# The first layer's gate and FFN modulation vectors in two 16-bit parts, through tiles of their own

## The chip, the cores and the metric

The kernel runs on one core of one Trainium2 chip. The metric is device time in microseconds (us) of one execution. Three runs of the kernel before gave 1661.7, 1661.75 and 1665.76 us; their median, 1661.75 us, is the time before.

## The reference, cut to what matters

Two models run one after the other: a two-layer block (a mixer and a convolutional FFN in each layer, with modulation vectors), and then a hybrid block. The change touches only the modulation vectors of the first layer (layer 0, the "even" one):

```python
mod_l = (jax.nn.silu(c) @ mod_w[layer] + mod_b[layer])[:, None, :]
mod_c = (jax.nn.silu(c_ctx) @ mod_w[layer] + mod_b[layer])[None, None, :]
sh1l, sc1l, g1l, sh2l, sc2l, g2l = jnp.split(mod_l, 6, axis=-1)
...
yc, yl = even_mixer(hc, hl, ...)
xl = xl + g1l * yl
hl = modulate(xl, norm_ffn_g[layer], sh2l, sc2l)
xl = xl + g2l * conv_ffn(hl, ...)
```

Of the six vectors, numbered r = 0 to 5, the first two shape the mixer's input. Vector 2 is the gate on the mixer's output, 3 and 4 are shift and scale of the FFN's norm, 5 is the gate on the FFN's output. Each is a product of two input vectors (latent and context) of 1024 with a 1024 x 1024 matrix in 32-bit floats: 4 MB of weights a vector.

## The kernel before, in words

**Weights.** Weights arrive in 32-bit floats as tiles `st` of 128 x 2048 (1 MB), by `load_w` (L313), whose loads stand on SP's queue one after the other. For the large products `get_w` (L318) makes two 16-bit parts of a tile: `whi` is its rounding to f16 on ACT (through `act`, L306), `wlo` the remainder in bf16, a subtraction on DVE or, with `eng=self.G`, on GpSimd (through `tt`, L294). A product is then three passes of 16-bit matmuls (L332).

**Modulation.** `mod_steps` (L487) computes one vector of one layer in four blocks b, each with one 1 MB tile. With `whole=True` a block is 16 matmuls in 32-bit floats directly on `st`, with the 32-column input `cs` (L505). The trace records each of these as two, so a vector has 64 records. Without `whole` the block goes through `get_w`, and 16 matmuls, 8 on `whi` and 8 on `wlo`, run with the input in three bf16 pieces, `c3`. After the four blocks the row is copied out (`mrow`, ACT), transposed by two small matmuls (L514) and added to the bias (`modc`, DVE). The four matmuls of one k go to four separate groups of 32 columns of PE.

**The first layer's mixer.** `layer0_mixer` (L538) opens three pools, `gp` (the linear attention), `ev` (`yf`, `mqk`, `vext`) and `mp` (the mLSTM's work tiles), runs the mixer, and closes them. What follows uses their space: `xT` (the residual), and the pool `tw`, which holds the output projection's weight parts and the four `st` tiles of vector 5. Pools are made with `reuse_waits="tile"`, so that a new tile waits for the old tiles under it only. Under the last tiles of `tw` and behind them lie `yf`, `vext` and the tiles of `mp`, which are read until the mLSTM's last head is done.

**Around the change.** Vectors 2, 3 and 4 are computed with `whole=True`, their `st` tiles from the pool `wst` (three tiles, on the other side of the memory, used by all weight loads). Behind them in the program come the projection `eo` (four blocks `even_o`, 96 matmuls of 512 columns for the first two and 192 of 256 columns for the others), whose results are multiplied by vector 2 and added to `xT` (L303, DVE), the FFN's norm, vector 5, and the FFN's first product `up`.

**The order.** Tile's scheduler orders the instructions of each engine at build time, with the program's order as priority: what stands later in the program fills places where earlier work isn't ready. Once built, each engine and SP's queue run in that fixed order. So the matmuls of vectors 2 to 4, which stand behind the mixer in the program, are spread between the matmuls of the mLSTM (`S` L943, `nd` L956, `msk` and `plain` L928 to L930).

Of the kernel before, what the change touches and what calls it, by code (L numbers as in the profile page):

```python
# [248 lines left out]
class Program:  # L249
# [288 lines left out]
    def layer0_mixer(self):  # L538
        h, I = self.h, self.I
        with ExitStack() as ph:  # L540
            gp = self.pool("gp", 1, None, ph)
            ev = self.pool("ev", 1, None, ph)
            mp = self.pool("mp", 1, None, ph)
            yf = ev.tile([128, 8, 512], F32, name="yf")
            mqk = ev.tile([128, 8, 512], F32, name="mqk")
            vext = ev.tile([128, 4, 4, 129], F32, name="vext")
            self.rows = [mp.tile([128, 512], F32, name=n) for n in ("li", "lf", "lb", "lm")]
            for t in self.rows:
                self.G.memset(t[:64], 0.0)
            self.G.memset(vext[:, :, :, 128:129], 1.0)  # L550
            self.gla(gp, h, I["even_w"], yf)
            self.mlstm_inputs(h, I["even_w"], mqk, vext, yf)
            for i in range(4):
                self.split(h[0][:, i], h[1][:, i], yf[:, i])
            self.mlstm(mp, h, mqk, vext, yf)
            self.dbg("ym", h[0])
        self.res2 = self.pool("res2")
        self.xT = self.res2.tile([128, 8, 512], F32, name="xT")
        self.nc.sync.dma_start(self.xT, I["xT"].rearrange("p (k t) -> p k t", k=8))
        with ExitStack() as tail:  # L560
            tw = self.pool("tw", 4, None, tail)
            for r in (2, 3, 4):
                for _ in self.mod_steps(0, r, whole=True):
                    pass
            w = [self.get_w(I["even_o"][b], 4, 512, parts=tw) for b in range(4)]

            for b in range(2):
                for c in range(4):
                    ps = self.mm("eo")
                    self.proj_fm(ps, w[b], c * 128, 128, h, 0, 512, nk=4)  # L570
                    self.add_residual(ps, 0, 2, 4 * b + c, BOTH)

            for s in range(2):
                for b in range(2):
                    for c2 in range(2):
                        ps = self.mm("eo")
                        for c in range(2):
                            self.proj_fm(ps[:, c * 256:c * 256 + 256], w[2 + b], (2 * c2 + c) * 128, 128, h,
                                         256 * s, 256 * s + 256, nk=4, h0=4)
                        for c in range(2):  # L580
                            self.add_residual(ps[:, c * 256:], 0, 2, 4 * b + 2 * c2 + c, ((s, 0, 256),), 256 * s)
                if s == 0:
                    self.norm_stream(0, 1, 0, "ml")
            for _ in self.mod_steps(0, 5, pool=tw, whole=True):
                pass
        self.dbg("xmid0", self.xT)
# [1404 lines left out]
```

## Time and profile before

| | |
|---|---|
| median of three runs | 1661.75 us |
| the profiled execution's own time | 1664.73 us |
| its span, first to last instruction | 1662.9 us |
| PE busy | 1578.0 us (95%) |
| DVE busy | 1207.7 us (73%) |
| ACT busy | 848.6 us (51%) |
| POOL (GpSimd) busy | 490.0 us (29%) |
| mean granted TensorE clock | 0.977 |

PE's busy time counts matmuls from the first to the last of a run of them, with modelled ends, so a busy PE can still wait inside. The stretch that the change touches lies between 254 and 340 us of the span: the mLSTM's last units, the mixer's end, and the projection `eo`.

### The profile page before, as it was taken

How to read it: one execution, taken by the hardware profiler on the slowest of the kernel's cores; microseconds unless marked ns; L12 is line 12 of the kernel's file. 1: busy time of each engine (PE TensorE's matmuls, PEld its weight loads, DVE VectorE, ACT ScalarE, POOL GpSimd, SP SyncE). 2: the span in 40 equal slices, each digit the busy share in tenths (PEclk: the TensorE clock that was granted, in tenths of full speed). 3: DMA queues.
4: the chain of work that ended last, by engine and by line, in shares of the span. 5: the costliest groups of instructions: out<-in, count | busy, mean ns of one | idle time of the engine just before them, and what ended most of it. 6: DMA issues, size and time to landing. Idle time of an engine off the chain costs nothing.

```text
span 1662.9 us, 31811 instructions
## 1 busy us (share of the span) xinstructions
PE 1578.0 (95%) x12978; PEld 1083.3 (65%) x12978; DVE 1207.7 (73%) x2626; ACT 848.6 (51%) x1390; POOL 490.0 (29%) x275
## 2 busy tenths in 40 slices
PE   6999999899999999999899999599999999999998
PEld 3555865477444444376565667488887787778877
DVE  6877845778877795556887988899976875366734
ACT  4745524435555544434665565366664644556542
POOL 0000000035878740001000100279944312431150
PEclk9999999999999999999999999899999989999999
DMA  9322126642433446632222314345454342333651
GB/s 389 106 82 78 53 77 243 245 177 99 158 133 135 137 138 222 202 124 78 93 88 77 127 55 149 113 171 204 140 194 168 139 166 102 138 129 108 228 178 52
DMA packets 41186, 236.77 MB, mean 142 GB/s; under 512 B 4688, under 2 KB 5456, under 8 KB 21200
## 3 DMA queue, kind: packets, MB, share of 16 engines
q1 hardware_dynamic: 41040, 234.74, 40.0%
q8 instruction: 102, 1.67, 0.4%
q14 instruction: 44, 0.36, 0.1%
HBM read 233.68 MB, written 1.05 MB: 141 GB/s over the span
## 4 chain that ended last, share of the span: by engine, by line
PE 75%; DVE 11%; DMA 5%; ACT 5%; issue 3%; POOL 1%; ACTq 0%; SPq 0%; DVEq 0%; POOLq 0%
PE up L332 19%; PE sx L332 5%; PE dn L332 4%; PE fm L332 4%; PE mg L332 4%; PE mqk L332 3%; PE br L332 3%; DVE wlo L294 3%; PE tm L339 2%; ACT whi L306 2%; DMA st<-in_mod_w_dram 2%; PE sz L332 2%; PE eo L332 2%; PE so L332 2%; PE sc L1654 2%
## 5 line engine op out<-in xcount | busy, mean ns | idle before, releaser
L332 PEld LDWEIGHTS <-whi 128*128 128x128 f16 (+2 forms) x5240 | 511.9, 99 | 253.9 <-issue 38.7
L294 POOL TENSOR_TENSOR wlo<-st,whi 128x1024 bf16<-128x1024 f32 (+2 forms) x112 | 356.8, 3196 | 915.9 <-ACT whi L306 814.5
L306 ACT ACTIVATE whi<-st 128x2048 f16<-128x2048 f32 (+3 forms) x242 | 369.7, 1536 | 268.2 <-PE up L332 44.8
L332 PEld LDWEIGHTS <-wlo 128*128 128x128 bf16 (+2 forms) x2620 | 258.9, 99 | 126.0 <-issue 13.2
L303 DVE SCALAR_TENSOR_TENSOR u<-up,fcw,u 128x189 f32<-128x189 f32 (+3 forms) x792 | 297.6, 430 | 50.8 <-ACT u L306 42.7
L294 DVE TENSOR_TENSOR wlo<-st,whi 128x2048 bf16<-128x2048 f32 (+3 forms) x130 | 255.0, 1965 | 87.9 <-ACT whi L306 83.0
L332 PE MATMUL up<-hh,whi 128*128 128x256 f16 (+1 forms) x752 | 239.4, 320 | 2.7 <-ACT hh L306 1.9
L332 PE MATMUL up<-hl,whi 128*128 128x256 bf16 (+1 forms) x752 | 238.9, 319 | 2.7 <-DVE hl L303 2.7
L332 PE MATMUL up<-hh,wlo 128*128 128x256 f16 (+1 forms) x752 | 238.7, 319 | 0.0
L332 PE MATMUL dn<-hidh,wlo 128*128 128x256 f16 (+1 forms) x396 | 122.4, 311 | 2.0 <-DVE wlo L294 2.0
L332 PE MATMUL dn<-hidh,whi 128*128 128x256 f16 (+1 forms) x396 | 122.3, 310 | 0.9 <-ACT whi L306 0.7
L332 PE MATMUL dn<-hidl,whi 128*128 128x256 bf16 (+1 forms) x396 | 122.3, 310 | 0.0
L306 ACT ACTIVATE u<-up,ppt,fcw 128x512 f32<-128x512 f32 (+1 forms) x88 | 57.9, 659 | 44.0 <-PE up L332 43.9
L332 PE MATMUL fm<-hh,whi 128*128 128x256 f16 x288 | 78.5, 273 | 0.5 <-DVE xc L303 0.5
L332 PE MATMUL fm<-hh,wlo 128*128 128x256 f16 x288 | 78.5, 273 | 0.0
L332 PE MATMUL fm<-hl,whi 128*128 128x256 bf16 x288 | 78.5, 273 | 0.0
L332 PE MATMUL mg<-hh,wlo 128*128 128x256 f16 x256 | 71.0, 277 | 3.6 <-POOL wlo L294 3.6
L332 PE MATMUL mg<-hl,whi 128*128 128x256 bf16 x256 | 70.9, 277 | 1.2 <-DVE hl L303 1.2
L332 PE MATMUL mg<-hh,whi 128*128 128x256 f16 x256 | 70.7, 277 | 0.9 <-ACT mgt L306 0.9
L298 POOL TENSOR_SCALAR E<-E,rs 128x128 f32<-128x128 f32 (+1 forms) x48 | 37.1, 787 | 111.6 <-DVE rs L1665 51.1
L339 PEld LDWEIGHTS <-hh 128*128 128x128 f16 x640 | 62.8, 101 | 10.0 <-issue 1.1
L294 POOL TENSOR_TENSOR sg<-sg,u 128x512 f32<-128x512 f32 (+1 forms) x44 | 46.6, 1059 | 27.0 <-ACT sg L306 26.7
(539 smaller groups left out, 3075.2 us busy)
## 6 DMA issues: line engine op xcount, KB each, us to landing
st<-in_w_up_dram SPq DMA_DIRECT2D x44, 1024.0 KB, 4.9
st<-in_w_dram SPq DMA_DIRECT2D x25, 1024.0 KB, 4.8
st<-in_mod_w_dram SPq DMA_DIRECT2D x48, 512.0 KB, 4.5
st<-in_w_dn_dram SPq DMA_DIRECT2D x32, 704.0 KB, 4.1
st<-in_ssd_w_dram SPq DMA_DIRECT2D x20, 1024.0 KB, 4.8
st<-in_mod_w_dram SPq DMA_DIRECT2D x16, 1024.0 KB, 5.0
st<-in_w_m_dram SPq DMA_DIRECT2D x32, 512.0 KB, 4.3
st<-in_even_w_dram SPq DMA_DIRECT2D x14, 1024.0 KB, 5.1
```

Of the source, the lines that this page charges most:

```text
L294: (eng or self.V).tensor_tensor(o, a, b, op=op)
L298: (eng or self.V).tensor_scalar(o, a, s1, None, op0=op0)
L303: self.V.scalar_tensor_tensor(o, a, s, b, op0=op0, op1=op1)
L306: self.S.activation(o, i, func, **kw)
L332: self.T.matmul(ps, w[a][:, k, c0:c0 + cw], h[b][:, h0 + k, t0:t1], start=first and k == 0 and i == 0, stop=last and k == nk - 1 and i == 2)
L339: self.T.matmul(ps, h[b][:, k, t0:t0 + 128], w[a][:, k, c0:c0 + cw], start=k == 0 and i == 0, stop=k == nk - 1 and i == 2)
L1654: T.matmul(ps[:, a:b], q[r, tb * 128:tb * 128 + 128], k[r, 0:b - a], start=True, stop=False)
```

## The change

Vectors 2, 3 and 4 leave the 32-bit path. Their 12 blocks go through `get_w` with a pool `tm` of their own, two tiles each of `st`, `whi` and `wlo` (8, 4 and 4 KB a partition), opened behind `tw`; `wlo` is made on GpSimd. `tm` lies on the space of the closed pools: its first `st` tile is on the end of `vext` and the start of `mp`, the other tiles on `mp`.

```diff
@@ -559,8 +559,9 @@
         with ExitStack() as tail:
             tw = self.pool("tw", 4, None, tail)
+            tm = self.pool("tm", 2, None, tail)
             for r in (2, 3, 4):
-                for _ in self.mod_steps(0, r, whole=True):
+                for _ in self.mod_steps(0, r, eng=self.G, pool=tm, parts=tm):
                     pass
             w = [self.get_w(I["even_o"][b], 4, 512, parts=tw) for b in range(4)]
```

The scheduler then orders the program anew. Three places show it; line numbers behind L559 are one higher in the changed kernel.

**PE, from the last mLSTM unit on.** `nd` is the last unit's product, `yT` the transposition of a head's result, `mod` the modulation (L505), `eo` the projection. Before:

```order
L505 MATMUL mod<-st,cs 32x256 x10
L956 MATMUL nd<-vext,W 128x129 x14
L505 MATMUL mod<-st,cs 32x256
L943 MATMUL S<-mqk 128x256
L919 MATMUL yT<-ept,hm 128x128 x4
L943 MATMUL S<-mqk 128x256
L514 MATMUL mod<-ept,mrow 128x8 x2
L956 MATMUL nd<-vext,W 128x129 x20
L919 MATMUL yT<-ept,hm 128x128 x4
L332 LDWEIGHTS whi
L332 MATMUL eo<-hh,whi 128x512
```

Of the change:

```order
L957 MATMUL nd<-vext,W 128x129 x17
L944 MATMUL S<-mqk 128x256
L920 MATMUL yT<-ept,hm 128x128 x4
L944 MATMUL S<-mqk 128x256
L957 MATMUL nd<-vext,W 128x129 x20
L920 MATMUL yT<-ept,hm 128x128 x8
L505 LDWEIGHTS c_99
L505 MATMUL mod<-whi,c_99 32x256
```

All 192 matmuls of the three vectors now stand behind the last `nd` and `yT`. The 128 of vectors 2 and 3, and the first 8 of vector 4, stand ahead of the first `eo`; the rest of vector 4 stands in groups of 16 and 12 between groups of 12 `eo`.

**SP's queue from the end of the mixer's weights on** (`in_mod_w` 128x2048 are modulation weights of layer 0, `in_mod_w` 128x1024 those of layer 1, `in_w_up` the FFN's). Before:

```order
L315 DMA st<-in_even_w_dram 128x2048 x9
L315 DMA st<-in_mod_w_dram 128x2048 x3
L559 DMA xT<-in_xT_dram 128x4096
L315 DMA st<-in_mod_w_dram 128x2048 x9
L315 DMA st<-in_even_o_dram 128x2048 x3
L315 DMA st<-in_mod_w_dram 128x2048 x4
L315 DMA st<-in_even_o_dram 128x2048
L315 DMA st<-in_w_up_dram 128x2048 x2
L315 DMA st<-in_mod_w_dram 128x1024 x2
```

Of the change:

```order
L315 DMA st<-in_even_w_dram 128x2048 x9
L315 DMA st<-in_even_o_dram 128x2048 x3
L559 DMA xT<-in_xT_dram 128x4096
L315 DMA st<-in_mod_w_dram 128x2048 x4
L315 DMA st<-in_even_o_dram 128x2048
L315 DMA st<-in_w_up_dram 128x2048 x2
L315 DMA st<-in_mod_w_dram 128x2048 x2
L315 DMA st<-in_w_up_dram 128x2048 x3
L315 DMA st<-in_mod_w_dram 128x2048 x2
L315 DMA st<-in_w_up_dram 128x2048
L315 DMA st<-in_mod_w_dram 128x2048 x8
```

In both, the group of four `in_mod_w` tiles ahead of the last `even_o` is vector 5. The 12 tiles of vectors 2 to 4 stood ahead of `even_o`; now they stand behind the fourth `even_o` and two `w_up` tiles, two, two and eight at a time.

**POOL's subtractions from its first on.** The numbers tell the tiles apart: `st_4520`, `st_4576` and `st_4632` are `w_up`, the others here are `tm`'s, in order. Before, the first row was `wlo` of `w_up` too, with the two `w_up` tiles followed by layer 1's modulation. Of the change:

```order
L294 TENSOR_TENSOR wlo_4523<-st_4520,whi_4522 128x2048
L294 TENSOR_TENSOR wlo_4579<-st_4576,whi_4578 128x2048
L294 TENSOR_TENSOR wlo_3667<-st_3664,whi_3666 128x2048
L294 TENSOR_TENSOR wlo_3689<-st_3686,whi_3688 128x2048
L294 TENSOR_TENSOR wlo_4635<-st_4632,whi_4634 128x2048
L294 TENSOR_TENSOR wlo_3711<-st_3708,whi_3710 128x2048
L294 TENSOR_TENSOR wlo_3733<-st_3730,whi_3732 128x2048
L294 TENSOR_TENSOR wlo_3761<-st_3758,whi_3760 128x2048
```

Fifteen subtractions of 128x2048 stand in a row: three of `w_up` and the 12 of the three vectors.

## Rows read from the trace of the kernel before

**Rows 1.** The page: busy time by engine, and the chain by engine.

```profile
PE 1578.0 (95%) x12978; PEld 1083.3 (65%) x12978; DVE 1207.7 (73%) x2626; ACT 848.6 (51%) x1390; POOL 490.0 (29%) x275
PE 75%; DVE 11%; DMA 5%; ACT 5%; issue 3%; POOL 1%; ACTq 0%; SPq 0%; DVEq 0%; POOLq 0%
```

**Rows 2.** Windows: busy us by engine, PE's clock, DMA share, GB/s.

```profile
254.00:300.00 46.00, 46.00 (x365) 26.68 (x364) 25.65 (x104) 19.02 (x64) 0.00 (x0) 1.00 0.68 252
300.00:313.00 13.00, 8.18 (x58) 6.70 (x56) 11.04 (x47) 6.64 (x22) 0.00 (x0) 1.00 0.25 83
375.00:392.00 17.00, 17.00 (x158) 15.19 (x156) 10.46 (x36) 4.71 (x11) 0.00 (x0) 1.00 0.01 2
```

**Rows 3.** The chain between 254 and 317 us: shares, then pieces (start, us).

```profile
by line: PE nd L956 27.3%; PE mod L505 23.8%; PE S L943 13.8%; DVE wlo L294 3.7%; DVE W L303 2.9%; ACT whi L306 2.9%; ACT W L306 2.7%; DVE hm L303 2.7%; PE msk L930 2.6%; PE msk L928 2.6%; PE msk L929 2.5%; PE plain L929 2.5%; PE plain L928
262.71 3.12 PE nd L956 x28
278.45 3.32 PE nd L956 x28
296.51 2.67 PE nd L956 x22
306.88 3.41 PE nd L956 x28
```

**Rows 4.** Timeline at the mixer's end: DVE's last read of `yf`, and SP.

```profile
311.95 0.69 DVE L303 SCALAR_TENSOR_TENSOR hm<-yf,hm 128x512 f32<-128x512 f32 x1
312.74 2.37 SPq L315 DMA_DIRECT2D st<-in_mod_w_dram  x4
317.46 0.33 SPq L315 DMA_DIRECT2D st<-in_even_o_dram  x1
319.74 2.60 SPq L315 DMA_DIRECT2D st<-in_w_up_dram  x2
```

**Rows 5.** Timeline behind it: ACT's casts and POOL's first subtraction.

```profile
328.17 1.91 ACT L306 ACTIVATE whi<-st 128x2048 f16<-128x2048 f32 x1 [9.46 <-DMA st<-in_even_o_dram]
330.67 1.91 ACT L306 ACTIVATE whi<-st 128x2048 f16<-128x2048 f32 x1
332.65 4.08 POOL L294 TENSOR_TENSOR wlo<-st,whi 128x2048 bf16<-128x2048 f32 x1 [295.94 <-ACT whi L306]
```

**Rows 6.** The price of a block elsewhere: POOL's subtraction, all of POOL's, DMA to landing.

```profile
513.87 4.08 POOL L294 TENSOR_TENSOR wlo<-st,whi 128x2048 bf16<-128x2048 f32 x1 [2.16 <-ACT whi L306]
L294 POOL TENSOR_TENSOR wlo<-st,whi x112: 2114/3306/4524, 332.7 to 1621.1; 128x2048 bf16<-128x2048 f32 x54, 128x1024 bf16<-128x1024 f32 x54, 128x1408 bf16<-128x1408 f32 x4
st<-in_mod_w_dram SPq DMA_DIRECT2D x16, 1024.0 KB, 5.0
```

**Rows 7.** PE's timeline: `eo` from its start to the last of 512 columns.

```profile
310.68 0.66 PE L919 MATMUL yT<-ept,hm 128*128 128x128 f32 x4 [0.41 <-DVE hm L303]
315.17 0.61 PE L332 MATMUL eo<-hh,whi 128*128 128x512 f16 x1 [3.83 <-ACT whi L306]
320.45 0.45 PE L332 MATMUL eo<-hh,whi 128*128 128x512 f16 x1
338.88 0.38 PE L332 MATMUL eo<-hl,whi 128*128 128x512 bf16 x1
339.09 0.38 PE L332 MATMUL eo<-hh,wlo 128*128 128x512 f16 x1
```

**Rows 8.** The chain behind: `up`, and eight 16-bit modulation matmuls of layer 1.

```profile
375.22 17.14 PE up L332 x157
392.36 0.33 PE mod L505 x8
```

## The prediction

> **What bounds the kernel now.** I read the page first: PE is busy 95% of the span and 75% of the chain is PE's, while POOL is busy 29% [rows 1]. An average says little about the stretch that the change touches, so I took the windows there [rows 2]. From 254 to 300 us PE is busy throughout, at full clock; the reader is to see DVE at 25.65 of 46 us and ACT at 19.02 beside it. From 300 to 313 us PE has 8.18 of 13 us and DVE 11.04: the last mLSTM unit is a dependence between engines. The chain of the stretch [rows 3] gives the modulation's matmuls 23.8% of 63 us, 15.0 us, all between 254 and 297. Last come the timelines at the mixer's end [rows 4, 5, 7]. They show an end mark: DVE reads `yf` for the last time until 311.95 + 0.69 = 312.64. I call this moment M. SP's next load starts at M + 0.1, and `eo` starts at M + 2.5.
>
> **What is removed: PE's 32-bit matmuls in the mixer.** 15.0 us of PE leave the chain, and 0.6 us of L514's. How much sooner does the mixer end? At most 15.6, if PE alone bounds. Nothing, if these matmuls only fill places where PE would wait. The rows lie between. The last products of a head start at 262.71, 278.45, 296.51 and 306.88 [rows 3]: units of 15.7 and 18.1 us with modulation in them, and a last one of 10.4 us without any, which has no successor beside it. Two units of 12 us would save 9.8 us. Against 254 to 300 in full: with 15 us gone, DVE's 25.65 us would fill 83% of what is left, about as dense as in the last unit (11.04 of 13, 85%), where dependences set the pace [rows 2]. I take **10 us**, nearer to the units' own rows, with 3 and 15.6 for the range. M moves from 312.6 to about 302.6.
>
> **What is added: a chain of 12 blocks behind M.** PE is in order, and 128 modulation matmuls now stand ahead of the first `eo`. `eo` can't start before the eighth block's `wlo`. Nothing of a block can start before M: `tm`'s loads stand on SP behind the fourth `even_o` and two `w_up` loads, each of which waits for a DVE subtraction that itself comes behind the mixer. I take their times from the same loads of before, M + 4.8, M + 7.1 and M + 9.4 (319.74 + 2.60 less the 0.33 of an issue) [rows 4]. The first two `tm` loads so start at M + 9.7, behind 4 MB of vector 5 and 3 MB more. But POOL is not ready for them anyway:
>
> - POOL's first `w_up` subtraction starts at M + 20.0 (332.65) [rows 5], as before, since what leads to it is the same. Then come `w_up`, two blocks, `w_up`, two blocks. Seven subtractions of 4.08 us [rows 6] end at M + 48.6, with block 4.
> - Block 5's `st` comes free with block 3's `wlo`, M + 44.5. Its load lands 5.0 us later [rows 6], and I add 0.1 since a `w_up` load runs ahead of it; ACT casts in 1.9 us [rows 5], POOL subtracts in 4.1: block 5 at M + 55.7, and block 6, loaded from M + 48.6, at M + 59.8 behind it.
> - From here two tiles of `st` set the pace: load, cast, subtraction and 0.1 for the handovers, 5.0 + 1.9 + 4.1 + 0.1 = 11.1 us for a pair of blocks. Blocks 7 and 8 end at M + 66.8 and M + 70.9, 9 and 10 at M + 77.9 and M + 82.0, 11 and 12 at M + 89.0 and M + 93.1.
> - PE's part is small. Eight 16-bit matmuls take 0.33 us [rows 8], a block 0.66, and only the last 0.35 of the last block lies on the path. ACT's 12 casts, 12 x 1.9 = 22.9 us, lie in the chain above; DVE gains nothing to do.
> - By M + 93.1 four groups of 12 `eo` have run between the blocks. 48 are left, at 339.09 - 338.88 = 0.21 us each: 10.1 us. PE has been idle most of the time, and so starts slow: after 3.83 us of idle time before, `eo` ran at 0.61 us a matmul until 320.45 instead of 0.38, half the clock for 5.3 us, which cost about 2.5 [rows 7]. End of the 512-column `eo`: 93.1 + 0.4 + 10.1 + 2.5 = M + 106.1.
>
> Before, the same `eo` end at 339.09 + 0.2 = 339.3, M + 26.7 [rows 7].
>
> **The sum.** 106.1 - 26.7 = 79.4 later, less the 10 by which M itself is earlier: 69.4, **70 us slower**. I see nothing behind that takes it back: the FFN's `up` runs from 375 to 392 with PE busy 17.00 of 17 us [rows 2, 8], so weights prepared longer ahead of it shorten nothing, and layer 1's modulation comes in the same lockstep as before. The sum was made in the profiled execution, whose 1664.73 us are 0.2% above the median of 1661.75; against the median it gives 1661.75 + 70 = 1732.
>
> **Two rules against the rows.** All of POOL's subtractions ran between 2.1 and 4.52 us [rows 6] over three widths; those of 2048 columns shown singly took 4.08 [rows 5, 6]. By the Trainium skill, "GPSIMD Engine Reference", section 3.1, a two-input operation of 2048 32-bit columns takes 4497 ns on GpSimd and 2293 ns on VectorE, and by the same page's section 8 it contends with VectorE's two-input instructions for its ports. By 4.5 instead of 4.08 the blocks would end about 12 x 0.4 = 5 us later, and the sum would be an estimated 75. The row decides for 4.08, since DVE has little to do while POOL works here.
>
> The clock after idle time is rows 7's. By the Trainium skill, "TensorE: Matmul & The Clock Gate", section "HAM oscillation — how this bites in real kernels", waits between bursts bring the half clock back every time. By it the `eo` between the blocks would run at half clock as well, which hides in POOL's time, and only the start of the last 48 counts, as in the sum.
>
> **The rivals.**
>
> *The blocks start before the mixer ends (faster).* A new tile waits only for the old tiles under it; if `tm`'s tiles came free early and loads and subtractions ran beside the mLSTM, PE would be rid of 15.6 us and `eo` would start as before: 1661.75 - 10 = 1652, at best 1646. It decides where block 8's `wlo` is done by M + 2.5, nearly 70 us sooner than above. For it speaks that POOL is idle in all of the mixer [rows 2, 5]. Against it: the tiles lie on `vext` and `mp`, read to the end, and SP's order holds them behind loads that start at M + 4.8 and later. Chance 0.03.
>
> *Loads are hidden, POOL alone is the bound.* Then 15 subtractions run without a gap from M + 20.0: 15 x 4.09 = 61.3, M + 81.3, 11.8 less than above: 58 slower, 1720. For this a load and a cast would have to fit beside one subtraction, 6.9 against 4.1 us [rows 5, 6]. If the mixer also ends the full 15.6 sooner, 1714. Chance 0.10.
>
> *POOL and PE are slower than their rows.* POOL at its largest 4.52 us [rows 6]: 5 us more; the last 48 `eo` all at half clock: 10.1 instead of 2.5 lost, 8 more; the mixer only 3 us sooner: 7 more. 70 + 20 = 90 slower, 1752. For it speaks that PE stops and starts twelve times here. Chance 0.14.
>
> *The time comes back behind, or the change does nothing.* If weight loads that now run ahead unblocked `up`, the end could be near 1662. The rows of `up` show no wait for weights [rows 8], and the built order does hold the 12 blocks. Chance 0.01.
>
> **How the numbers follow.** The forecast, 60 to 80 us slower, has a chance of 0.72. The range adds the near halves of POOL alone and of slower engines: 1715 to 1748. About 0.3%, 5 us, is what a measurement here can tell from no change. Faster by more: 0.03, the first rival. Within: 0.01. Slower: 0.96.
>
> **What would show it.** In the profile after: no L505 on `st` before 300 us, units of about 12 us in the mLSTM and M near 303; then PE nearly idle for some 70 us with its clock at half, and 15 POOL subtractions of 4.1 us, first without gaps, then two to every 11 us; the first `eo` at about M + 73. It is wrong if a `tm` load starts before M, if the pairs come closer than 10 us, or if `up` starts less than 55 us later than at 375.

## The result, and the profile after

Four runs of the changed kernel gave 1717.34 to 1732.42 us, median **1723.33 us**; four of the kernel before 1661.7 to 1665.84, median 1663.76. The ratio is 1.0361, with a 95% interval of 1.0329 to 1.0392: 60 us slower. The forecast was 1732, range 1715 to 1748. The profiled execution of the changed kernel took 1720.71 us, its span is 1718.8 us.

The page of the changed kernel, busy time by engine and the chain by engine, against [rows 1]:

```profile
PE 1565.8 (91%) x12912; PEld 1080.9 (63%) x12978; DVE 1204.8 (70%) x2626; ACT 871.5 (51%) x1402; POOL 539.6 (31%) x287
PE 70%; DVE 13%; ACT 5%; DMA 5%; issue 4%; POOL 3%; ACTq 0%; SPq 0%; DVEq 0%; POOLq 0%
```

POOL's busy time grew by 49.6 us, 12 subtractions of 4.1, as it had to. The number to see is its share of the chain, 1% before and 3% now. The chain between 254 and 440 us gives POOL's subtractions 17.8%, 33 us in which the end of the kernel waits for one of them. An engine's busy time says nothing of this.

The windows, with the columns of [rows 2]:

```profile
254.00:290.00 36.00, 31.04 (x172) 20.60 (x172) 27.12 (x110) 19.77 (x68) 0.00 (x0) 1.00 0.01 1
303.00:375.00 72.00, 14.11 (x148) 8.48 (x150) 9.72 (x15) 29.41 (x18) 47.81 (x12) 0.50 0.77 290
```

The mixer's end has lost the full PE of [rows 2], and its DMA share is 0.01: nothing is loaded beside it any more. Behind it stand 72 us in which PE works 14.11 us at a granted clock of 0.50, the lower of its two levels (1.2 of 2.4 GHz), while POOL works 47.81. That second row is the result.

DVE's last read of `yf` and SP's queue behind it, against [rows 4]:

```profile
297.88 0.69 DVE L303 SCALAR_TENSOR_TENSOR hm<-yf,hm 128x512 f32<-128x512 f32 x1
298.65 1.98 SPq L315 DMA_DIRECT2D st<-in_mod_w_dram  x4
305.67 2.60 SPq L315 DMA_DIRECT2D st<-in_w_up_dram  x2
308.32 0.90 SPq L315 DMA_DIRECT2D st<-in_mod_w_dram  x2
```

M is now 297.88 + 0.69 = 298.57, 14.07 us sooner than before. The first two tiles of `tm` are asked for at 308.32, M + 9.75. All of POOL's timeline up to the 12th block:

```profile
318.08 28.18 POOL L294 TENSOR_TENSOR wlo<-st,whi 128x2048 bf16<-128x2048 f32 x7 [280.01 <-ACT whi L306]
349.28 8.08 POOL L294 TENSOR_TENSOR wlo<-st,whi 128x2048 bf16<-128x2048 f32 x2 [3.03 <-ACT whi L306]
360.36 8.08 POOL L294 TENSOR_TENSOR wlo<-st,whi 128x2048 bf16<-128x2048 f32 x2 [3.00 <-ACT whi L306]
371.53 8.09 POOL L294 TENSOR_TENSOR wlo<-st,whi 128x2048 bf16<-128x2048 f32 x2 [3.09 <-ACT whi L306]
382.50 8.10 POOL L294 TENSOR_TENSOR wlo<-st,whi 128x2048 bf16<-128x2048 f32 x2 [2.89 <-ACT whi L306]
```

Seven subtractions without a gap, and then pairs that start 11.0 to 11.2 us apart with 3 us of idle time ahead of each. The bracket names ACT as the releaser, but ACT had itself waited. The chain of waits between 254 and 440 us shows one period whole:

```profile
338.18 4.07 POOL wlo L294
342.26 4.93 DMA st<-in_mod_w_dram
347.29 1.92 ACT whi L306
349.28 1.79 POOL wlo L294
```

Subtraction, load into the tile that it freed, cast, subtraction: the two `st` tiles in turn. Last, PE's `eo` against [rows 7], and the first long piece of `up` in the chain against [rows 8]:

```profile
373.19 0.59 PE L332 MATMUL eo<-hh,whi 128*128 128x512 f16 x1 [0.33 <-DVE modc L294]
386.62 0.29 PE L505 MATMUL mod<-wlo,c 128*32 128x256 bf16 x4 [1.16 <-POOL wlo L294]
391.09 0.39 PE L332 MATMUL eo<-hh,whi 128*128 128x512 f16 x1
402.39 0.38 PE L332 MATMUL eo<-hh,wlo 128*128 128x512 f16 x1
437.13 16.81 PE up L332 x154
```

`eo` starts at M + 74.6, the 512-column `eo` end at 402.6, M + 104.0, and that piece of `up` starts 61.9 us later than at 375.22. The first matmul of `up` is a sharper mark than the end: 368.4 us before, 430.0 now, 61.6 later. Behind it the ten profiled executions of this study take between 1284.5 and 1295.3 us to the end of their spans, in no order that follows the size of the edit's effect. So a median can be off by some us in either direction, and the mark is used beside the medians below.

### The profile page after: what moved, and what is told of

It is laid out like the page before. It is cut to its first block, busy times and chain, and to the rows that moved or that the text cites. A ratio compares the mean times of both kernels' runs of the same rounds, so it can differ in the third digit from the quotient of the medians.

```text
span 1718.8 us, 31781 instructions
## 1 busy us (share of the span) xinstructions
PE 1565.8 (91%) x12912; PEld 1080.9 (63%) x12978; DVE 1204.8 (70%) x2626; ACT 871.5 (51%) x1402; POOL 539.6 (31%) x287
## 4 chain that ended last, share of the span: by engine, by line
PE 70%; DVE 13%; ACT 5%; DMA 5%; issue 4%; POOL 3%; ACTq 0%; SPq 0%; DVEq 0%; POOLq 0%
PE up L332 17%; PE dn L332 7%; PE sx L332 5%; PE fm L332 4%; POOL wlo L294 3%; PE mg L332 3%; DVE u L303 3%; ACT whi L306 3%; PE sz L332 2%; DVE wlo L294 2%; PE br L332 2%; PE so L332 2%; PE eo L332 2%; DMA st<-in_w_m_dram 2%; PE tm L339 2%
## 5 line engine op out<-in xcount | busy, mean ns | idle before, releaser
L294 POOL TENSOR_TENSOR wlo<-st,whi 128x1024 bf16<-128x1024 f32 (+2 forms) x124 | 405.8, 3284 | 926.6 <-ACT whi L306 822.0
L306 ACT ACTIVATE whi<-st 128x2048 f16<-128x2048 f32 (+3 forms) x254 | 392.9, 1555 | 293.2 <-DMA st<-in_mod_w_dram 62.0
L332 PE MATMUL up<-hl,whi 128*128 128x256 bf16 (+1 forms) x733 | 230.4, 316 | 3.5 <-DVE hl L303 3.5
L332 PE MATMUL dn<-hidl,whi 128*128 128x256 bf16 (+1 forms) x384 | 117.0, 306 | 0.0
L505 PEld LDWEIGHTS <-c 128*32 128x32 bf16 x576 | 13.9, 101 | 83.7 <-issue 83.0
```

The lines of the kernel that those rows point to most:

```text
L294: (eng or self.V).tensor_tensor(o, a, b, op=op)
L306: self.S.activation(o, i, func, **kw)
L332: self.T.matmul(ps, w[a][:, k, c0:c0 + cw], h[b][:, h0 + k, t0:t1], start=first and k == 0 and i == 0, stop=last and k == nk - 1 and i == 2)
L505: T.matmul(ps[32 * j:32 * j + 32, :256], c[:, 2 * b + k], w[:, 0 if halves else k, 256 * j:256 * j + 256], start=b == k == i == 0, stop=b ...
```

## The experiments

The runs of the kernel before on the same chips had medians of 1663.8 (the first four experiments), 1665.1 (the next three) and 1663.4 us (the last). What they gave, with M and the first matmul of `up` from the traces:

| kernel | median us | ratio (95%) | M | first `up` |
|---|---|---|---|---|
| before | 1663.8 | 1 | 312.6 | 368.4 |
| the change | 1723.3 | 1.0361 (1.0329 to 1.0392) | 298.6 | 430.0 |
| 1, `wlo` on DVE | 1715.7 | 1.0306 (1.0248 to 1.0363) | 297.0 | 421.1 |
| 2, four half tiles | 1717.0 | 1.0310 (1.0238 to 1.0382) | 299.0 | 422.7 |
| 3, the place alone | 1706.2 | 1.0249 (1.0186 to 1.0312) | 297.1 | 411.9 |
| 4, the parts alone | 1680.5 | 1.0105 (1.0041 to 1.0168) | 328.5 | 391.5 |
| 5, the parts alone, DVE | 1671.6 | 1.0046 (1.0026 to 1.0067) | 320.4 | 377.4 |
| 6, vectors left out | 1645.2 | 0.9897 (0.9860 to 0.9935) | 296.6 | 352.1 |
| 7, two vectors behind `eo` | 1691.6 | 1.0173 (1.0141 to 1.0205) | 302.0 | 398.7 |
| 8, casts only | 1667.1 | 1.0019 (0.9990 to 1.0049) | 314.9 | 371.8 |

The diffs are against the changed kernel, in 5 and 8 against experiment 4's. The theory: the tiles' **place** puts a chain of 12 blocks behind M, and the two `st` tiles pace it, load, cast and subtraction one behind the other. The rivals: POOL's rate alone is the bound; the place alone costs it all; the parts alone do.

### 1. The subtraction on DVE

```diff
-                for _ in self.mod_steps(0, r, eng=self.G, pool=tm, parts=tm):
+                for _ in self.mod_steps(0, r, pool=tm, parts=tm):
```

> The same pool and order, wlo of the 12 blocks on DVE instead of GpSimd. Theory (two st tiles set the pace: load, cast, subtraction one behind the other, and POOL only through its 4.07 us): a pair of blocks takes 4.93 + 1.91 + 2.29 + 0.1 = 9.2 us instead of the 11.1 of the changed kernel, and the first two blocks no longer queue behind POOL's w_up, so the 12th ends near M + 74 instead of M + 92: about 18 us less than the changed kernel, 1705 us (1698 to 1712). Rival 1 (the rate of the subtracting engine alone is the bound): 12 x 2.29 = 27.5 us behind M + 25, M + 52, about 40 us less, 1683 us. Rival 2 (the place alone, whatever engine subtracts): no change, 1723 us. Periods between subtractions in the trace tell: 9.2 us a pair, 4.6 us a pair, or 11.1 us a pair.

Measured: 1715.68 us, outside the range. Pieces of the chain show two periods:

```profile
337.38 4.91 DMA st<-in_mod_w_dram
342.37 1.92 ACT whi L306
344.31 2.30 DVE wlo L294
346.63 4.81 DMA st<-in_mod_w_dram
351.55 1.92 ACT whi L306
353.49 2.30 DVE wlo L294
```

344.31, 353.49, then 362.72 and 371.93: 9.2 us a pair, as the theory has it. Both rivals' periods, 4.6 and 11.1, are out. The 12th block ends at 377.2, M + 80.2, not M + 74. The first pair was late, and its timeline shows why:

```profile
321.46 7.49 DVE L294 TENSOR_TENSOR wlo<-st,whi 128x2048 bf16<-128x2048 f32 x2 [5.19 <-ACT whi L306]
327.00 5.88 POOL L294 TENSOR_TENSOR wlo<-st,whi 128x2048 bf16<-128x2048 f32 x1 [2.39 <-ACT whi L306]
```

Two subtractions of 2.29 us on DVE took 7.49 while POOL worked on `w_up`, and one of 4.07 on POOL took 5.88 while DVE worked. I had not expected that the two engines hold each other up; experiment 4 shows it at length. The next pair was another 1.3 us late, as its load took 6.24 us. The last group of 12 `eo` ahead of the 12th block's matmuls then started only at 375.07, behind a DVE addition to `xT` that itself stood behind the 11th block's subtraction, and at half clock it took 4.31 us in place of 2.6. So the 512-column `eo` ended 16.5 us behind the 12th block, where the change has 12.0. These 6.2 and 4.5 us, less 1.6 by which M is sooner, are what is missing at `up`, which starts 8.9 us sooner than in the change where 18 were expected.

### 2. Four tiles of half the width

```diff
-            tm = self.pool("tm", 2, None, tail)
+            tm = self.pool("tm", 4, None, tail)
...
-                for _ in self.mod_steps(0, r, eng=self.G, pool=tm, parts=tm):
+                for _ in self.mod_steps(0, r, eng=lambda: self.G, pool=tm, parts=tm, halves=True):
```

> The same 32 KB a partition, but as four tiles of 1024 columns instead of two of 2048, wlo on GpSimd. Theory: with four tiles in turn a load (4.4 us to landing for 512 KB) and a cast (1.05) fit beside three subtractions of about 2.1 to 2.3 us, so POOL runs without gaps: 24 x 2.2 + 3 x 4.08 = 65 us behind M + 19.5, the last block at M + 84.5 instead of M + 92: 7 to 8 us less than the changed kernel, about 1716 us (1711 to 1720). This is what the prediction's second rival (POOL alone the bound) needs in order to hold. Rival (the loads' rate is the bound, not their turn with two tiles): gaps between POOL's subtractions stay, no change, 1723 us or more.

Measured: 1716.98 us, and 7.3 us less at `up`. POOL's timeline is one row for everything:

```profile
318.42 62.26 POOL L294 TENSOR_TENSOR wlo<-st,whi 128x2048 bf16<-128x2048 f32 x27 [279.97 <-ACT whi L306]
```

27 subtractions (three of `w_up`, 24 halves) without a gap, ended at M + 81.7. With four tiles the prediction's second rival is true, and POOL alone is the bound; with the change's two tiles it is not. The difference between the two is the 3 us ahead of each of the change's last four pairs, 12.0 us, less 1.7 that the halves take longer in all: the chain ends 10.3 us sooner.

### 3. The place alone

```diff
-                for _ in self.mod_steps(0, r, eng=self.G, pool=tm, parts=tm):
+                for _ in self.mod_steps(0, r, pool=tm, whole=True):
```

> The 32-bit path of the kernel before (no cast, no subtraction), but its st tiles from the pool on the closed mixer pools' space: the place alone. Theory (the blocks can't begin before DVE's last read of yf, and each pair of tiles waits for its use): M as in the changed kernel, 14 us sooner than before; a pair takes 4.93 us of load and up to 2.5 us of matmuls at half clock, 7.5 us, six pairs from M + 10 end at M + 55 instead of M + 92: 38 us less than the changed kernel, about 1685 us (1675 to 1697), still 11 to 35 us slower than the kernel before. Rival 1 (casts and subtractions are the whole cost, the place nothing): 1664 - 14 = 1650 us. Rival 2 (the place is the whole cost): 1723 us.

Measured: 1706.15 us, above the range: without any cast or subtraction the place still costs 43.5 us at `up`, more than two thirds of the change's 61.6. Pieces of the chain, and the windows (columns as in [rows 2]; the last three are PE's clock, DMA share and GB/s):

```profile
306.83 12.62 DMA st<-in_mod_w_dram
319.50 1.98 PE mod L505 x16
321.49 7.93 DMA st<-in_mod_w_dram
...
331.47 8.38 DMA st<-in_mod_w_dram
...
341.88 4.80 DMA st<-in_mod_w_dram
```

```profile
303.00:340.00 37.00, 9.97 (x76) 4.14 (x80) 8.05 (x12) 8.86 (x7) 12.14 (x3) 0.50 1.01 422
```

I had put 4.93 us on every load. That held for the next two on the chain (4.80 and 4.81 us), whose pairs came 6.8 and 6.9 us apart; a last one took 5.91. From 303 to 340 all 16 DMA engines were busy (1.01) at 422 GB/s, since vector 5, `even_o`, `w_up` and the moved 12 MB are all wanted at once. The first loads on the chain took 12.62, 7.93 and 8.38 us there, 14 us more in all than I had put. The place alone thus has a second cost: it moves 12 MB out of a stretch where little else is loaded (DMA share 0.01 in the change) into one where DMA is full.

### 4. The parts alone

```diff
-            tm = self.pool("tm", 2, None, tail)
...
-                for _ in self.mod_steps(0, r, eng=self.G, pool=tm, parts=tm):
+                for _ in self.mod_steps(0, r, eng=self.G):
```

> The 16-bit parts with wlo on GpSimd, but in the shared pools that the other weights use, so the loads can run beside the mixer: the parts alone. Theory (the place is what lets the chain show): the matmuls stand among the mixer's again, eo follows the mixer at once as in the kernel before, PE's modulation in the mixer falls from 15.0 to about 192 x 0.33 / 8 = 7.9 us, while ACT gains 12 x 1.9 = 23 us there beside its 19 of 46 us: between 7 us faster and 11 us slower than the kernel before, 1663 us (1655 to 1675), 50 us or more less than the changed kernel. Rival (12 subtractions of 4.07 us on GpSimd cost about their sum wherever they stand): 1700 us or more.

Measured: 1680.53 us, 43 less than the change, so the place is the larger part. But it is above the theory's range, and M is at 328.5, 16 us later than before, though PE's modulation fell from 18.31 us (window 240 to 312 of the kernel before) to 12.07 (240 to 330 here, the same 204 records). A vector's 64 records of the 32-bit path are 32 matmuls, eight a block and not 16 as I wrote in the description of the kernel. Two groups of DVE's instructions between 200 and 330 us, here:

```profile
L294 DVE TENSOR_TENSOR den<-den,guard 128x2 f32<-128x2 f32 x14 | 14.1, 1005 | 0.0
L298 DVE TENSOR_SCALAR den<-den 128x2 f32<-128x2 f32 x13 | 11.8, 907 | 0.3
```

and in the kernel before:

```profile
L298 DVE TENSOR_SCALAR den<-den 128x2 f32<-128x2 f32 x16 | 2.6, 167 | 0.2
L294 DVE TENSOR_TENSOR den<-den,guard 128x2 f32<-128x2 f32 x16 | 2.5, 157 | 9.3 <-ACT den L306 8.9
```

The same instructions on two columns take 5.4 and 6.4 times as long on average. DVE's and POOL's timelines beside each other say when:

```profile
269.92 3.47 DVE L294 TENSOR_TENSOR den<-den,guard 128x2 f32<-128x2 f32 x1
273.63 3.78 DVE L298 TENSOR_SCALAR den<-den 128x2 f32<-128x2 f32 x1
282.01 0.17 DVE L294 TENSOR_TENSOR modc<-mod,ept 128x16 f32<-128x16 f32 x1 [1.22 <-PE mod L514]
287.29 3.94 DVE L303 SCALAR_TENSOR_TENSOR r<-rt,r 128x4 f32<-128x4 f32 x1
309.86 0.69 DVE L847 TENSOR_REDUCE hss<-hsq 128x4 f32<-128x512 f32 x1 [0.47 <-ACT hsq L306]
```

```profile
265.27 12.11 POOL L294 TENSOR_TENSOR wlo<-st,whi 128x2048 bf16<-128x2048 f32 x3 [4.35 <-ACT whi L306]
280.78 4.06 POOL L294 TENSOR_TENSOR wlo<-st,whi 128x2048 bf16<-128x2048 f32 x1 [3.40 <-ACT whi L306]
287.14 4.07 POOL L294 TENSOR_TENSOR wlo<-st,whi 128x2048 bf16<-128x2048 f32 x1 [2.30 <-ACT whi L306]
309.39 8.09 POOL L294 TENSOR_TENSOR wlo<-st,whi 128x2048 bf16<-128x2048 f32 x2 [2.37 <-PE nd L956]
```

POOL's three subtractions from 265.27 end at 269.3, 273.4 and 277.4. DVE's `den` ends at 273.39, the next held one at 277.41, and `r` at 291.23 against POOL's 291.21: each held instruction ends with POOL's. Not all are held. While POOL ran, `modc`, one of whose two inputs is PE's result `mod`, took 0.17 us and the reduction `hss`, with one input, 0.69. By the Trainium skill, "SBUF — State Buffer", section "Who interferes with whom", GpSimd shares a pair of ports with VectorE under an exclusive lock that whoever issues first keeps for its whole instruction: a VectorE instruction with two SBUF inputs, or a one-input one in a two-port mode, which `tensor_scalar` can enter, is blocked until a GpSimd instruction that reads SBUF is done, and `tensor_reduce` never is. The trace agrees in every row above, and experiment 5 tests it.

### 5. The parts alone, subtracted on DVE

```diff
-                for _ in self.mod_steps(0, r, eng=self.G):
+                for _ in self.mod_steps(0, r):
```

> As the run with the parts in the shared pools (1680.53 us, M at 328.5), but wlo of the 12 blocks on DVE: the same 12 casts on ACT, 12 x 2.29 = 27.5 us more on DVE, nothing on POOL inside the mixer. Theory (GpSimd's subtractions hold up DVE: in that run a den of 0.16 us took 3.0 to 3.8 us and ended with POOL's subtraction): DVE's small instructions keep their 0.16 us, the mixer ends at least 8 us sooner, M between 306 and 320, time 1656 to 1672 us, in spite of more work on DVE. Rival (the casts on ACT and the longer way from load to matmul slow the mixer): M stays at 328 or later, 1680 us or more; with 27.5 us of DVE added to a full DVE up to 1690 us.

Measured: 1671.59 us, M at 320.4. DVE has 27.5 us more to do, and the mixer ends 8.1 us sooner than with POOL:

```profile
L298 DVE TENSOR_SCALAR den<-den 128x2 f32<-128x2 f32 x16 | 2.5, 165 | 0.1
L294 DVE TENSOR_TENSOR den<-den,guard 128x2 f32<-128x2 f32 x16 | 2.4, 157 | 2.9 <-ACT den L306 2.8
```

The small instructions are back at 157 and 165 ns. The hold-up was real: it cost 8.1 us at M, 14.1 at `up`, and 8.9 between the two medians. But M is 0.4 us past the theory's range: against the kernel before, 7.8 us remain that POOL doesn't explain.

### 6. The three vectors left out

```diff
-            tm = self.pool("tm", 2, None, tail)
...
-                for _ in self.mod_steps(0, r, eng=self.G, pool=tm, parts=tm):
-                    pass
+                self.V.memset(self.modc[0][:, r], 0.5)
+            self.stt(self.modA[0][:, 1], self.modc[0][:, 4], 1.0, bc(self.ng[1][:, 0], 1, 2), ALU.add, ALU.mult)
```

> Vectors 2, 3 and 4 left out: their rows are set to a constant, with no loads, casts, subtractions or matmuls. It measures by itself what the mixer gains when its 15.0 us of 32-bit matmuls go, and what the tail costs without any chain. Theory: M at 297 to 299 as in the changed kernel (14 to 15.6 us sooner than 312.6), eo at M + 2.5 and ended at M + 26.7 as before, so 14 to 16 us less than the kernel before: 1649 us (1644 to 1654); the chain of 12 blocks then costs 1723 - 1649 = 74 to 77 us. Rival (the mixer's end is freed but the time is lost again behind, in weights that come later than eo): over 1655 us.

Measured: 1645.17 us. M is 296.6, 16.0 us sooner, and `up` starts 16.3 us sooner: what the mixer gains reaches `up` whole. So a version of these three vectors has about 16 us to gain at `up`; the ratio of 0.9897 says 17 us of 1665, its interval 11 to 23. And the changed kernel's chain costs 430.0 - 352.1 = 77.9 us against having none.

### 7. Shift and scale behind the first `eo`

```diff
-            for r in (2, 3, 4):
-                for _ in self.mod_steps(0, r, eng=self.G, pool=tm, parts=tm):
-                    pass
+            for _ in self.mod_steps(0, 2, whole=True):
+                pass
...
+            for r in (3, 4):
+                for _ in self.mod_steps(0, r, eng=self.G, pool=tm, parts=tm):
+                    pass
             for s in range(2):
```

> Vector 2 on the 32-bit path in the mixer as before; vectors 3 and 4 through tm on GpSimd as in the changed kernel, but called behind the 512-column eo, so that no eo of 512 columns stands behind their matmuls on PE. Theory (a chain of 8 blocks that ends at M + 71 as in the changed kernel, whose end now holds the 256-column eo and the norm in place of the first eo): M about 10 us sooner than before, the 512-column eo ended near M + 27, the last eo some 10 us behind block 8, at M + 82 instead of M + 50: 32 less 10, about 22 us slower than the kernel before, 1686 us (1677 to 1696). Rival 1 (only PE's order held eo; behind it the chain is covered by eo): 1655 to 1664 us. Rival 2 (each block costs its share wherever it is called, 8 of 12): 1664 + 40 = 1704 us.

Measured: 1691.61 us, in the theory's range. M came 10.7 us sooner for two of three vectors. POOL's last pair and DVE's `sq` (of the FFN's norm) beside it:

```profile
364.80 8.27 POOL L294 TENSOR_TENSOR wlo<-st,whi 128x2048 bf16<-128x2048 f32 x2 [2.86 <-ACT whi L306]
365.06 8.29 DVE L294 TENSOR_TENSOR sq<-sq,s 128x256 f32<-128x256 f32 x2 [0.27 <-ACT s L306]
```

Block 8 ends at 373.07, M + 71.1, against the M + 71 expected and the M + 69.9 of the changed kernel: the chain's end hangs on M and the number of blocks, not on what PE does beside it. But `up` is 30.3 us late, not 22, since the last `eo` ran until M + 90.7. In the row of `sq`, two instructions that take 0.95 us for both once POOL is quiet took 8.29 beside POOL's 8.27: the hold-up of experiment 4, and the chain runs through both of them. The next 24 `eo` start behind them, at 374.19, at half clock (5.29 us, where the 24 after that take 2.79).

### 8. Casts without subtractions

```diff
-                terms = [(self.c3, w) for w in self.get_w(src, 2, 1024, eng, pool, parts)]
+                if l == 0 and r in (2, 3, 4):
+                    st = self.load_w(src, 2048, pool)
+                    hi = self.wsp.tile([128, 2048], F16, tag="whi", name="whi")
+                    self.act(hi, st)
+                    terms = 2 * [(self.c3, hi.rearrange("p (k n) -> p k n", k=2))]
+                else:
+                    terms = [(self.c3, w) for w in self.get_w(src, 2, 1024, eng, pool, parts)]
```

> As the run with the parts in the shared pools, with the 12 subtractions left out: the matmuls that should read wlo read whi again, so loads, casts and the number of 16-bit matmuls stay and only the remainder is not computed. The mixer ended at 312.6 us before, at 320.4 with the subtractions on DVE and at 328.5 with them on GpSimd. Theory (the subtractions are what slows the mixer, on DVE by its load, on GpSimd by holding DVE up): without them PE's saving shows, 18.3 us of modulation against about 9 to 10.6, M between 302 and 309, time 1650 to 1661 us. Rival (the 12 casts on ACT, 23 us, or the longer way from load to matmul): M between 316 and 321, time 1667 us or more.

Measured: 1667.05 us (1654.78 to 1671.29), no difference from before that can be told, and M at 314.9, between the theory's 302 to 309 and the rival's 316 to 321. Neither holds alone; the median is the rival's. PE's saving doesn't show even without subtractions, and two windows say what stands in its place:

```profile
260.00:280.00 20.00, 16.77 (x182) 10.74 (x182) 10.35 (x42) 19.39 (x33) 0.00 (x0) 1.00 0.88 321
280.00:300.00 20.00, 16.29 (x92) 9.32 (x93) 10.08 (x41) 9.64 (x26) 0.00 (x0) 0.74 0.38 153
```

The second stretch in the kernel before:

```profile
280.00:300.00 20.00, 20.00 (x162) 11.75 (x161) 11.51 (x47) 9.14 (x30) 0.00 (x0) 1.00 0.67 256
```

ACT is busy 19.39 of 20 us, with the casts between the mixer's own `W` and `hm`, while PE has 3.2 us idle; the chain there runs through two loads, of 5.73 and 6.48 us. From 280 to 300 us PE's granted clock is 0.74 where the kernel before has 1.00: between 283.80 and 294.40 PE is busy 9.96 of 10.60 us at 0.52, close to its lower level. Two `S` of 512 columns took 1.91 us there and 1.02 at 266.20, so by my estimate the slow clock puts M some 5 us later here. Experiments 4 and 5 have it too, with 0.70 and 0.78 from 280 to 300; experiment 6 has 0.83 there, where its mixer ends. This leaves a ladder for the mixer's end: 296.6 without the vectors, 312.6 with 32-bit matmuls, 314.9 with casts, 320.4 with DVE's subtractions, 328.5 with GpSimd's.

No version tried here that does the whole work beats the kernel before; experiment 5 comes nearest, at 1.0046. Experiments 6 and 8 leave part of the work out.

## Why the prediction was right

**The shape held step by step.** POOL's first `w_up` came at M + 19.5 (forecast 20.0), its seventh subtraction ended at M + 47.7 (48.6), blocks 5, 8 and 12 at M + 54.8, 69.9 and 92.0 (55.7, 70.9, 93.1), in pairs of 11.1 us. `eo` started at M + 74.6 (73). The sum was 69.4 us later at the end of the 512-column `eo`; it is 402.6 - 339.3 = 63.3. The 6.1 us between them are three terms of one sign, so none hides another:

- **The mixer's gain was mis-sized**: 10 us taken, 14.07 measured, inside the 3 to 15.6 given. The step that failed is the argument that dependences would set the pace once the matmuls were gone, drawn from the last unit. The traces say otherwise: 10.7 us for two vectors (experiment 7), 13.6 to 16.0 in the five kernels that take all three out. Where nothing takes their place, the 15.6 us of matmuls come back nearly whole, and the window with PE at 46.00 of 46 us [rows 2] was the better guide.
- **The chain ended 1.1 us sooner**, mostly from POOL's earlier start (0.5) and from seven subtractions of 4.03 us where 4.08 was taken (0.4).
- **The cost of a slow clock wasn't paid**, which took the rest, 1.0 us after the last block: 2.5 us were not lost, but 1.1 went to L514 and a wait for `xT`, and 0.3 to 48 matmuls of 0.216 us where 0.21 was taken. The step said that PE would start slow on its last 48 `eo`. PE did start slow, at 373.19 (0.59 us a matmul), but by 376.9 it was at 0.38, and the groups of 12 between blocks 9 and 12 left waits of 1.16 us at most, so that the last 48 began at 0.39. Of the rule of the Trainium skill, "TensorE: Matmul & The Clock Gate", section "HAM oscillation — how this bites in real kernels", that was weighed there, this trace shows one side only: waits of 20.7 us in all for `whi` and 30.0 for `wlo` between 303 and 375 went with a clock of 0.50, and waits of 0.42 to 1.16 us from 377 to 391 with 1.00.

**At the end of the run** 59.6 us are left between the medians, against 61.6 at `up`, within the spread behind `up`.

**The rules weighed.** 4.03 to 4.08 us for a subtraction held (one of its inputs has 16 bits), not the 4497 ns that the Trainium skill, "GPSIMD Engine Reference", section 3.1, gives for 32-bit inputs. The same page's contention, section 8, cost the change nothing that its trace shows: DVE is busy 9.72 of 72 us there, and what it does beside POOL keeps its length (`modc` 0.17 us, two `xT` 0.88). That it costs time elsewhere (8.1 us at M in experiment 4) is experiments 1, 4, 5 and 7.

**The rivals.** The blocks didn't start before M. POOL alone was not the bound, but was with four tiles (experiment 2), where the chain ended at M + 81.7 against the M + 81.3 of that rival and `up` came 7.3 us sooner. Slower engines did not come, and little came back behind: 63.3 us at the end of these `eo`, 61.6 at `up`. The decision between place and parts, which the prediction had not to make, is experiments 3 and 4: the place costs 43.5 us at `up` with the parts away, the parts 23.1 with the place away; both together 61.6.

**What stays open.** How much of PE's lost saving in experiment 8 is ACT's casts, how much the loads on its chain and how much the slow clock was not tried apart. The place brings three things together that no run separates: the wait for M, two tiles where `wst` has three, and SP's new order (the first `tm` load, at 308.32, starts as the two `w_up` ahead of it end, 305.67 + 2.60). Nor was it tried whether the 5.5 us of DVE's subtractions in the mixer are DVE's load or the matmuls' wait for `wlo`.

## What to carry to other kernels

Before giving loads a pool of their own on closed pools' space, look up when the old tiles under it are read last: that moment, not the pool's opening, is the earliest at which the work can start, and work that ran hidden beside the old phase then stands as a chain between two phases, at the pace of a load, a cast and a subtraction per turn of its buffers. Multiply that pace by the blocks and compare it with what the old path cost PE, here 11.1 us a pair, six pairs, against 15 us in all. And an idle engine is not free room: GpSimd was at 0% in the mixer, and its two-input operations there held up DVE's smallest instructions to about twenty times their length.

## What the runs showed of the hardware that was not expected

- A GpSimd subtraction of 4.07 us on 2048 columns held DVE instructions of 0.15 to 0.17 us for 2.6 to 3.9 us, until it ended (experiment 4). The profile counts the hold as DVE's busy time (`den` 1005 ns on average against 157), so a DVE that looks full may be waiting.
- The hold goes both ways: a GpSimd subtraction took 5.88 us beside DVE's (experiment 1).
- A 1 MB load on the chain took 4.8 us with room, and 7.9 to 12.6 us where the DMA engines moved 422 GB/s with a busy share of 1.01 (experiment 3).
- PE's granted clock fell inside the mixer in the kernels with casts there: 0.74 from 280 to 300 us in experiment 8, 0.78 in 5 and 0.70 in 4, against 1.00 in the kernel before.
